# Second mixer: k and b by token in diagonal blocks, and the convolution norm's sums at a later place

## The chip, the cores and the metric

The kernel runs on one core of a Trainium2 chip. The time is the device time of one execution in microseconds (us); the median of several runs is given. A profile of one execution shows what each engine did: TensorE (PE, its weight loads PEld), VectorE (DVE), ScalarE (ACT), GpSimd (POOL) and SyncE (SP), which issues most transfers.

## What is computed

Two transformer blocks over 512 tokens of 1024 channels, and then a third block whose mixer has two branches. The change lies in that mixer. Its branches, cut to what matters:

```python
# branch 1, by head of 64 channels, 16 heads; state S is 64 x 64
S_t = S_{t-1} diag(w_t) + (S_{t-1} (-kk_t)) (kk_t * a_t)^T + v_t k_t^T ;  o_t = S_t r_t
# branch 2: depthwise convolution over 31 tokens, layer norm over the channels, silu
u = glu[..., :1024] * sigmoid(glu[..., 1024:])
u = conv(u, conv_w) + conv_b                      # (512, 1024)
mu = mean(u, -1); var = mean(square(u - mu), -1)
c_out = silu((u - mu) * rsqrt(var + 1e-5) * g + b)
merged = gate0 * (a_out @ w_rwkv_proj) + gate1 * (c_out @ w_conv_proj)
```

## The kernel before

Everything is kept by channel: a tile is 128 channels by 512 tokens, and the mixer goes over 8 such blocks of channels, fc = 0 to 7, two heads in each. `second_mixer` is a software pipeline of nine stages: in stage i, `wkv_proj` of block i (products with `w_in`), `wkv_inputs` of i-1 (decays, k, b), `wkv_inverse` of i-2 and `wkv_chunks` of i-3 are cut into pieces by `yield`, and `interleave` takes the next piece of whichever part is furthest behind its rate. Beside them stand in `branches` the convolutions (`conv_chunk`, eight in stages 0 to 6), the gates (`branch_gate`) and, in stage 8, the convolution's norm and the first of its output products (`conv_out`). A scheduler behind this moves instructions within each engine's queue; so the order on an engine isn't quite that of the code, and every engine and every queue takes its instructions in that order.

`wkv_chunks` solves the recurrence by chunks of 64 tokens, eight steps for a block. A step makes s0 = KA v + AR S (`pair`, two half-array products of 64 x 64, one for each head), sa = `MD` s0 (L1661, a full product: MD holds both heads' inverse in diagonal blocks, zeros beside them), and the next state from k v + b sa (L1667, L1668, two pairs on `ktk` and `btk`, which lie head by head, 64 wide). The outputs gather in `po`: KA v, AR S and, at the step's end, UA sa (L1677). VectorE takes s0, sa and the state out of PSUM between these products.

`wkv_inverse` makes MD: four half-array products per chunk around an inverse of 16 x 16 blocks on VectorE (L1563 to L1568), whose operand goes out to memory (`ud`) and comes back (`ub`), as its result does (`md`, `mn`). Behind it k, b and v are transposed to lie by token (L1586 to L1598).

The convolution's norm: `ConvNorm.add` sums the blocks on GpSimd into `cnsum` and writes them to memory (`cod`). In stage 7 the generator `sums` takes the mean by a product with ones (L1350), then for each of 8 blocks `center`: load into a tile `cacc` of two buffers, subtract on GpSimd (L1357), store (L1358), square on ScalarE (L1359), add into `cnsq` on GpSimd (L1363). `var` is a product with ones again (L1368), a square root and a reciprocal. Both products use the PSUM bank `psd`, which the gates use too. In stage 8 `norm` loads each block again, scales it and writes it over H, the mixer's input, as soon as the gates have read that.

Of the kernel before, what the change touches and what calls it, by code (L numbers as in the profile page):

```python
# [11 lines left out]
F32 = mybir.dt.float32  # L12
# [1112 lines left out]
def second_mixer(g, outer):  # L1125
    nc, tc, d = g.nc, g.tc, g.d
    H = g.X
    with ExitStack() as st:
# [25 lines left out]
        with ExitStack() as s2, ExitStack() as s3, ExitStack() as s4:  # L1154
# [14 lines left out]

            MD = [k1.tile([128, 8, 128], F32, name=f"md{i}") for i in range(2)]  # L1170
            for t in MD:
                nc.gpsimd.memset(t, 0.0)
            parts = [{"MD": MD[i % 2]} for i in range(8)]

# [4 lines left out]
            def sums():  # L1179
                yield 0.0  # L1180
                cn.mean()
                yield 4.0
                for j in range(8):
                    cn.center(j, ka)
                    yield 1.0
                cn.var()

# [15 lines left out]
            def lora():  # L1203

                new = lambda tag, n, bufs: k1.tile([128, n], F32, name=tag, tag=tag, bufs=bufs)
                for blk in range(2):
                    raw = new("ua", 1024, 2).rearrange("p (k n) -> p k n", k=8)
                    nc.sync.dma_start(raw, d["lora1"][:, blk * 128:blk * 128 + 128].rearrange("(k p) n -> p k n", p=128))
                    pss = []
                    for sc in (omm[:, 24:48], vv("mu_lora")):  # L1210
                        w = new("ka", 1024, 2)
                        ws = w.rearrange("p (k n) -> p k n", k=8)
                        for i, (c0, c1) in ((0, (0, 64)), (1, (64, 128))) if blk == 0 else ((2, (0, 128)),):
                            s8 = sc[:, i * 8:i * 8 + 8].unsqueeze(2).to_broadcast([128, 8, c1 - c0])
                            nc.vector.tensor_tensor(ws[:, :, c0:c1], raw[:, :, c0:c1], s8, op=ALU.mult)
                        hi = g.whi.tile([128, 1024], F32R, name="whi", tag="whi")
                        lo = g.wlo.tile([128, 1024], F32R, name="wlo", tag="wlo")
                        split_sb(g, w, hi, lo)
                        ps = g.ps("pst")
                        for kc in range(8):  # L1220
                            o = slice(kc * 128, kc * 128 + 128)
                            mm3(nc, ps, (hi[:, o], lo[:, o]), (H[0][:, kc, :], H[1][:, kc, :]), kc == 0, kc == 7)
                            yield 0.65
                        pss.append(ps)
                    pre, sb = new("oo", 512, 1), new("gate", 512, 1)
                    nc.scalar.copy(sb, pss[1])
                    nc.vector.tensor_copy(pre[:, 0:1], pss[0][:, 0:1])
                    nc.vector.tensor_tensor(pre[:, 1:512], pss[0][:, 1:512], sb[:, 0:511], op=ALU.add)
                    if blk == 0:
                        nc.scalar.activation(pre[0:64], pre[0:64], AF.Tanh)  # L1230
                        for T, o in ((TW, 0), (TA, 64)):
                            own, oth = slice(o, o + 64), slice(64 - o, 128 - o)
                            nc.scalar.activation(T[own], pre[own], AF.Copy)
                            nc.vector.tensor_tensor(T[oth], pre[own], T[own].bitcast(F32), op=ALU.subtract)
                    else:
                        nc.scalar.activation(pre, pre, AF.Tanh, scale=0.5)
                        nc.vector.tensor_scalar(pre, pre, 0.5, 0.5, op0=ALU.mult, op1=ALU.add)
                        split_sb(g, pre, TG[0], TG[1])

            interleave((30.2, wkv_proj(g, 0, parts[0], env)), (16.0, branches(0)), (11.7, lora()))  # L1240
            for i in range(1, 9):
# [5 lines left out]
                if i == SUMS:  # L1247
                    work += [(12.7, sums())]
                interleave(*late, *work[::-1], (n, branches(i)))
# [72 lines left out]
class ConvNorm:  # L1322


    def __init__(self, g, k1, hv, ka):
        self.g, self.hv, self.pool = g, hv, None
        self.early = itertools.cycle([(ka, "cacc", 2), (ka, "cacc", 2), (ka, "glt", 1), (ka, "glu", 1), (ka, "r", 2), (ka, "k", 2)])
        self.sum = k1.tile([128, 512], F32, name="cnsum")
# [24 lines left out]
    def center(self, j, ka):  # L1353
        nc = self.g.nc
        t = ka.tile([128, 512], F32, name="cn", tag="cacc", bufs=2)
        nc.sync.dma_start(t, self.row(j))
# [35 lines left out]
def conv_chunk(g, fc, ka, vv, cw, H, cn):  # L1392
# [11 lines left out]
                         bias=vv("conv_b")[:, fc:fc + 1])  # L1404
    acc = ka.tile([128, 512], F32, name="cacc", tag="cacc", bufs=2)
    for j in range(1, 31):
# [29 lines left out]
def wkv_inputs(g, fc, st, env):  # L1436
# [43 lines left out]
    nc.scalar.activation(kk, k, AF.Copy, scale=col(vv("k_k"), fc))  # L1480
    sq = tmp("tmpa")
    nc.gpsimd.tensor_tensor(sq, kk, kk, op=ALU.mult)
# [8 lines left out]
    nc.vector.reciprocal(rs, rs)  # L1491
    BK = two("bk", (128, 2, 512), 2)
    b = BK[:, 0, :]
# [20 lines left out]
def wkv_inverse(g, fc, st, env):  # L1514
# [72 lines left out]
    for src, nm in ((st["v"], "vtk"), (BK[:, 0, :], "btk"), (BK[:, 1, :], "ktk")):  # L1587
        ps = g.ps("pst")
        for i in range(4):
            nc.tensor.transpose(ps[:, i * 128:i * 128 + 128], src[:, i * 128:i * 128 + 128], g.ident)  # L1590
        t = new(nm, (128, 8, 64), 2)
        p4 = ps.rearrange("p (i h f) -> p i h f", i=4, h=2)
        tv = t.rearrange("p (i e) f -> p i e f", e=2)
        for cp in range(2):
            for hp in range(2):
                nc.scalar.copy(tv[64 * hp:64 * hp + 64, :, cp, :], p4[64 * cp:64 * cp + 64, :, hp, :])
        tok.append(t)
        yield 0.5  # L1598
    bc = lambda m: m.unsqueeze(1).to_broadcast([128, 8, 64])
    for j in (4, 5):  # L1600
# [10 lines left out]
        if j == 5:  # L1611
            for hp in range(2):
                o = slice(64 * hp, 64 * hp + 64)
                nc.vector.tensor_tensor(st["MD"][o, :, o], c3(ps)[o], M[o], op=ALU.add)
        else:
# [12 lines left out]
def wkv_chunks(g, fc, st, env, A=None):  # L1628
# [6 lines left out]
    two = lambda tag, shape=(128, 512), bufs=1: kb.tile(list(shape), F32, name=tag, tag=tag, bufs=bufs)  # L1635
    AR, UA, KA, MD, F, bon = (st[k] for k in ("AR", "UA", "KA", "MD", "F", "bon"))
    gate = new("gate")
# [7 lines left out]
    St = None  # L1645
    sm = lambda tag: k1.tile([128, 64], F32, name=tag, tag=tag, bufs=3)
    pq = lambda: g.ps("psq")[:, 0:64]
    for cc in range(8):
        oc = po[:, cc * 64:cc * 64 + 64]
        ps = pq()  # L1650
        pair(nc, ps, KA[:, cc, 0, :], vt[:, cc, :], True, St is None)
        if St is not None:
            pair(nc, ps, AR[:, cc, 0, :], St, False, True)
        s0 = sm("s0")
        nc.vector.tensor_copy(s0, ps)
        pair(nc, oc, KA[:, cc, 1, :], vt[:, cc, :], True, False)
        if St is not None:
            pair(nc, oc, AR[:, cc, 1, :], St, False, False)
        yield 0.5
        ps = pq()  # L1660
        nc.tensor.matmul(ps, MD[:, cc, :], s0, start=True, stop=True)  # L1661
        sa = sm("sa")
        nc.vector.tensor_scalar_mul(sa, ps, col(st["rs"], cc))
        yield 0.4
        if cc < 7:
            ps = pq()
            pair(nc, ps, kt[:, cc, :], vt[:, cc, :], True, False)  # L1667
            pair(nc, ps, bt[:, cc, :], sa, False, True)  # L1668
            S2 = sm("st")
# [6 lines left out]
            St = S2  # L1676
        pair(nc, oc, UA[:, cc, 1, :], sa, False, True)  # L1677
        yield 0.5


# [18 lines left out]
    for k in range(4):  # L1699
        nc.tensor.transpose(ps[:, k * 128:k * 128 + 128], t[:, k * 128:k * 128 + 128], g.ident)  # L1700
    o = new("oo")
    p4 = ps.rearrange("p (i h f) -> p i h f", i=4, h=2)
# [55 lines left out]
```

## Time and profile before

| what | value |
|---|---|
| median of 3 runs | 2481.47 us (2478.55 to 2486.14) |
| the profiled execution | 2481.95 us |
| its span | 2479.8 us |
| mean granted TensorE clock | 0.984 |
| TensorE, VectorE, ScalarE, GpSimd busy | 95%, 60%, 52%, 42% |

The span reaches from the first to the last instruction of the profile. Of an instruction on the timeline the trace gives its start, its duration, and in brackets how long its engine stood idle ahead of it and what ended that. Matmuls are pipelined: what one costs is read from the distance between two starts, not from its duration. An fp32 product is shown as two passes, so a `pair` has "x4".

### The profile page before, as it was taken

To read this page: it belongs to the slowest core of one execution; us is meant where nothing else is said; L and a number is where in the kernel's file an instruction comes from. 1 tells how busy PE (TensorE), PEld (TensorE's weight loads), DVE (VectorE), ACT (ScalarE), POOL (GpSimd) and SP (SyncE) were. 2 spreads that over 40 slices of the span, in tenths; PEclk is the share of its full clock that TensorE was granted. 3 is DMA by queue.
4 is the path that set the end of the run, shared out by engine and by line. 5 is a ranking of instruction groups with operands and counts; after the bars stand their busy time and mean duration, and the time that the engine had idled before them with its cause. 6 is when DMAs were issued, how large, how long until landed. Compare 5 with 4: busy or idle time off the path is not lost.

```text
span 2479.8 us, 36415 instructions
## 1 busy us (share of the span) xinstructions
PE 2364.9 (95%) x14140; PEld 1898.6 (77%) x14140; DVE 1481.9 (60%) x2782; ACT 1283.0 (52%) x2005; POOL 1030.6 (42%) x571
## 2 busy tenths in 40 slices
PE   8999999999999999999999999999988999899998
PEld 6779778787777787877777877777766679787786
DVE  3776565666443655564685587877756542645556
ACT  5774454445465645444455454666655533544443
POOL 1114677662111025767632232323253114476772
PEclk9999999999999999999999999999998999999999
DMA  7445232347565244232372576666664468232322
GB/s 209 94 141 166 85 116 71 115 121 172 140 136 117 62 124 121 71 119 86 103 202 85 118 167 146 147 144 150 134 173 119 124 172 248 77 102 85 119 81 73
DMA packets 302349, 312.19 MB, mean 126 GB/s; under 512 B 61280, under 2 KB 234976, under 8 KB 302048
## 3 DMA queue, kind: packets, MB, share of 16 engines
q1 hardware_dynamic: 280432, 239.60, 31.9%
q0 software_dynamic: 21168, 68.17, 15.2%
q8 instruction: 111, 1.82, 0.3%
q10 hardware_dynamic: 576, 2.10, 0.2%
q14 instruction: 62, 0.51, 0.1%
HBM read 221.47 MB, written 20.19 MB: 97 GB/s over the span
## 4 chain that ended last, share of the span: by engine, by line
PE 55%; POOL 13%; issue 11%; DVE 9%; DMA 6%; ACT 6%; SPq 0%; POOLq 0%; DVEq 0%; ACTq 0%
PE psm L290 7%; PE psm L291 7%; PE psm L292 7%; POOL wlo L389 4%; PE psa L290 4%; PE psa L291 4%; PE psa L292 4%; POOL wlo L273 3%; DMA wlo<-wraw 2%; PE pst L1416 2%; PE psd L290 2%; PE pss L292 2%; PE pss L291 2%; PE pss L290 2%; PE psd L292 2%
## 5 line engine op out<-in xcount | busy, mean ns | idle before, releaser
L290 PE MATMUL psm<-xT,whi 128*128 128x512 f32 (+1 forms) x1192 | 476.2, 400 | 23.3 <-ACT hf L440 12.3
L292 PE MATMUL psm<-xT,wlo 128*128 128x512 f32 (+1 forms) x1192 | 469.7, 394 | 5.4 <-DMA wlo<-wraw 5.4
L291 PE MATMUL psm<-xT,whi 128*128 128x512 f32 (+1 forms) x1192 | 471.0, 395 | 0.5 <-DVE xT L352 0.5
L267 ACT ACTIVATE whi<-wraw 128x1024 fp32r<-128x1024 f32 (+3 forms) x287 | 285.7, 1005 | 290.8 <-PE psa L292 101.5
L271 POOL DMA_DIRECT2D wlo<-wraw x147 | 127.3, 872 | 729.0 <-ACT wlo L270 497.4
L273 POOL TENSOR_TENSOR wlo<-wraw,whi 128x1024 fp32r<-128x1024 f32 x122 | 315.5, 2620 | 102.0 <-ACT whi L267 73.4
L389 POOL TENSOR_TENSOR wlo<-wraw,whi 128x1024 fp32r<-128x1024 f32 x84 | 212.9, 2534 | 241.9 <-ACT whi L388 241.9
L290 PEld LDWEIGHTS psm<-xT,whi 128*128 128x128 f32 x1192 | 226.7, 190 | 74.7 <-ACT hf L440 13.6
L292 PEld LDWEIGHTS psm<-xT,wlo 128*128 128x128 f32 x1192 | 226.6, 190 | 53.1 <-DMA wlo<-wraw 6.5
L291 PEld LDWEIGHTS psm<-xT,whi 128*128 128x128 f32 x1192 | 227.4, 191 | 44.6 <-DVE xT L352 0.9
L290 PE MATMUL psa<-whi,hh 128*128 128x512 f32 x600 | 239.0, 398 | 15.6 <-DVE x L460 15.5
L291 PE MATMUL psa<-wlo,hh 128*128 128x512 f32 x600 | 236.6, 395 | 0.0
L292 PE MATMUL psa<-whi,hl 128*128 128x512 f32 x600 | 236.4, 395 | 0.0
L388 ACT ACTIVATE whi<-wraw 128x1024 fp32r<-128x1024 f32 x147 | 151.7, 1053 | 123.9 <-PE psa L292 61.8
L1407 DVE SCALAR_TENSOR_TENSOR psc<-glu,cw,psc 128x512 f32<-128x512 f32 x232 | 173.8, 749 | 5.9 <-ACT psc L1403 2.2
L388 ACT ACTIVATE hh<-hf 128x768 fp32r<-128x768 f32 (+1 forms) x96 | 87.8, 914 | 145.2 <-DVE hf L451 143.4
L389 DVE TENSOR_TENSOR hl<-hf,hh 128x768 fp32r<-128x768 f32 (+1 forms) x96 | 124.3, 1295 | 60.2 <-ACT hh L388 60.2
L290 PEld LDWEIGHTS psa<-whi,hh 128*128 128x128 f32 x600 | 112.8, 188 | 49.7 <-DVE x L460 23.1
L389 DVE TENSOR_TENSOR wlo<-wraw,whi 128x1024 fp32r<-128x1024 f32 x63 | 86.4, 1396 | 92.5 <-ACT whi L388 87.8
L270 ACT ACTIVATE wlo<-whi 128x1024 fp32r<-128x1024 f32 (+3 forms) x147 | 140.1, 956 | 2.3 <-PE psm L292 0.7
L292 PEld LDWEIGHTS psa<-whi,hl 128*128 128x128 f32 x600 | 112.8, 188 | 27.2 <-DVE hl L389 0.7
L291 PEld LDWEIGHTS psa<-wlo,hh 128*128 128x128 f32 x600 | 112.8, 188 | 25.8
(464 smaller groups left out, 5208.6 us busy)
## 6 DMA issues: line engine op xcount, KB each, us to landing
wlo<-wraw POOLq DMA_DIRECT2D x123, 512.0 KB, 5.3
wraw<-in_w_up SPq DMA_DIRECT2D x64, 512.0 KB, 4.5
wraw<-in_w_down SPq DMA_DIRECT2D x64, 512.0 KB, 3.6
wraw<-in_w_ff SPq DMA_DIRECT2D x64, 512.0 KB, 3.8
wraw<-in_w_in SPq DMA_DIRECT2D x56, 512.0 KB, 4.9
wraw<-in_od_w_in SPq DMA_DIRECT2D x24, 512.0 KB, 4.3
wraw<-in_ple_w_gate SPq DMA_DIRECT2D x16, 512.0 KB, 4.6
brow<-in_rows SPq DMA_DIRECT2D x13, 512.0 KB, 6.7
```

The lines of the kernel that those rows point to most:

```text
L267: nc.scalar.activation(hi[:, :m], raw[:, :m], AF.Copy)
L270: nc.scalar.activation(lo[:, :m], hi[:, :m].bitcast(F32), AF.Copy, scale=-1.0)
L271: nc.gpsimd.dma_start(lo[:, :m].bitcast(F32), raw[:, :m], accum_op=ALU.add)
L273: eng.tensor_tensor(lo[:, :m], raw[:, :m], hi[:, :m].bitcast(F32), op=ALU.subtract)
L290: nc.tensor.matmul(ps, w[0], x[0], start=first, stop=False)
L291: nc.tensor.matmul(ps, w[0], x[1], start=False, stop=False)
L292: nc.tensor.matmul(ps, w[1], x[0], start=False, stop=last)
L388: g.nc.scalar.activation(hi, src, AF.Copy)
L389: (eng or g.nc.gpsimd).tensor_tensor(lo, src, hi.bitcast(F32), op=ALU.subtract)
L1407: nc.vector.scalar_tensor_tensor(acc if j == 30 else part, u[:, j:j + 512], cw[:, fc * 31 + j:fc * 31 + j + 1], part, op0=ALU.mult, op1=AL ...
L1416: nc.tensor.matmul(ps[o], lhs[o], rhs[o], start=start, stop=stop)
```

## The change

The k and b tiles by token become 128 x 128 diagonal blocks with zeros beside them, kept in two sets as MD is; the products k v and b sa become one full product each. UA sa moves from the end of a step into the next step, behind its AR S products. The pieces of a step are yielded at 0.7, 0.3 and 0.4 instead of 0.5, 0.4 and 0.5. `sums` begins later (a first yield of 2.0), its rate becomes 17.5 and `var` stands 3.0 behind the last block. For space, `cacc` gets one buffer, the small tiles two, `oo` becomes `ot`, and the square of kk lies in `bk`. Line numbers behind L1170 grow by one, and those behind L1592 by two to four.

```diff
-            MD = [k1.tile([128, 8, 128], F32, name=f"md{i}") for i in range(2)]
-            for t in MD:
+            diag = {k: [k1.tile([128, 8, 128], F32, name=f"{k}{i}") for i in range(2)] for k in ("md", "btk", "ktk")}
+            for t in itertools.chain(*diag.values()):
                 nc.gpsimd.memset(t, 0.0)
-            parts = [{"MD": MD[i % 2]} for i in range(8)]
+            parts = [{k: t[i % 2] for k, t in diag.items()} for i in range(8)]
...
             def sums():
-                yield 0.0
+                yield 2.0
                 cn.mean()
                 yield 4.0
                 for j in range(8):
                     cn.center(j, ka)
                     yield 1.0
+                yield 3.0
                 cn.var()
...
-                    work += [(12.7, sums())]
+                    work += [(17.5, sums())]
...
-        self.early = itertools.cycle([(ka, "cacc", 2), (ka, "cacc", 2), (ka, "glt", 1), (ka, "glu", 1), (ka, "r", 2), (ka, "k", 2)])
+        self.early = itertools.cycle([(ka, "cacc", 1), (ka, "glt", 1), (ka, "glu", 1), (ka, "r", 2), (ka, "k", 2)])
...
-        t = ka.tile([128, 512], F32, name="cn", tag="cacc", bufs=2)
+        t = ka.tile([128, 512], F32, name="cn", tag="cacc")
...
-    sq = tmp("tmpa")
+    BK = two("bk", (128, 2, 512), 2)
+    sq = BK[:, 1, :]
...
-        t = new(nm, (128, 8, 64), 2)
+        t = st.get(nm) or new(nm, (128, 8, 64), 2)
...
-                nc.scalar.copy(tv[64 * hp:64 * hp + 64, :, cp, :], p4[64 * cp:64 * cp + 64, :, hp, :])
+                o = slice(64 * hp, 64 * hp + 64)
+                nc.scalar.copy(tv[o, :, cp, o if nm in st else slice(0, 64)], p4[64 * cp:64 * cp + 64, :, hp, :])
...
-    sm = lambda tag: k1.tile([128, 64], F32, name=tag, tag=tag, bufs=3)
+    sm = lambda tag: k1.tile([128, 64], F32, name=tag, tag=tag, bufs=2)
...
         if St is not None:
             pair(nc, ps, AR[:, cc, 0, :], St, False, True)
+            pair(nc, oc(cc - 1), UA[:, cc - 1, 1, :], sa, False, True)
...
-        yield 0.5
+        yield 0.7
...
-        yield 0.4
+        yield 0.3
         if cc < 7:
             ps = pq()
-            pair(nc, ps, kt[:, cc, :], vt[:, cc, :], True, False)
-            pair(nc, ps, bt[:, cc, :], sa, False, True)
+            nc.tensor.matmul(ps, kt[:, cc, :], vt[:, cc, :], start=True, stop=False)
+            nc.tensor.matmul(ps, bt[:, cc, :], sa, start=False, stop=True)
...
             St = S2
-        pair(nc, oc, UA[:, cc, 1, :], sa, False, True)
-        yield 0.5
+            yield 0.4
+    pair(nc, oc(7), UA[:, 7, 1, :], sa, False, True)
...
-    o = new("oo")
+    o = t
```

How this moves instructions, at three places. First TensorE around the mean product, which stood behind the second step's b product of the fifth chunk loop:

```order
L1416 MATMUL psq<-vtk,ktk 64x64 x2
L1416 MATMUL psq<-sa,btk 64x64 x2
L1350 MATMUL psd<-cnsum,ca 128x512
L1416 MATMUL pso<-sa,ua 64x64 x2
L1416 MATMUL pso<-vtk,ka 64x64 x2
```

and now stands behind the last step's AR S product (L1671 and L1672 are the full products on k and b):

```order
L1671 MATMUL psq<-vtk,ktk_11250 128x64
L1672 MATMUL psq<-sa,btk_11248 128x64
L291 MATMUL psd<-xT_62,whi 128x512
L292 MATMUL psd<-xT_61,wlo 128x512
L290 MATMUL psm<-xT_61,whi 128x512
L291 MATMUL psm<-xT_62,whi 128x512
L292 MATMUL psm<-xT_61,wlo 128x512
L1417 MATMUL psq<-vtk,ka 64x64 x2
L1417 MATMUL psq<-st,ar 64x64 x2
L1351 MATMUL psd<-cnsum,ca 128x512
L1417 MATMUL pso<-sa,ua 64x64 x2
L1417 MATMUL pso<-vtk,ka 64x64 x2
```

Six steps of the loop have moved ahead of the mean. Second TensorE around the variance product, before, with the sixth chunk loop (its first step's L1661) behind it:

```order
L1416 MATMUL pst<-mm,yy 64x64 x16
L1416 MATMUL pst<-ar,bk 64x128 x8
L1368 MATMUL psd<-cnsq,ca 128x512
L1661 MATMUL psq<-s_16718,md_11247 128x64
L1474 MATMUL psm<-ta,whi 128x512
```

and now, with that loop's last step (L1665 on `md`), the products of the seventh inverse and then the gates (`psd`, L290 to L292):

```order
L1665 MATMUL psq<-s_17069,md_11247 128x64
L1417 MATMUL pso<-sa,ua 64x64 x2
L1417 MATMUL psq<-vtk,ka 64x64 x2
L1417 MATMUL pso<-vtk,ka 64x64 x2
L1417 MATMUL pst<-mn,ua 64x64 x16
L1703 MATMUL pst<-ca,ot 128x128 x4
L1417 MATMUL pst<-mn,yy 64x64 x16
L1417 MATMUL pst<-yy,mn 64x64 x16
L1417 MATMUL pst<-nn,ua 64x64 x16
L1369 MATMUL psd<-cnsq,ca 128x512
L1417 MATMUL pst<-mm,yy 64x64 x12
L290 MATMUL psd<-xT_61,whi 128x512
```

The whole sixth loop now stands ahead of the variance, with no 512-column product in it. Third SyncE's queue, where the centred blocks were loaded (L1356) and stored (L1358) in twos:

```order
L1356 DMA cn<-cod 128x512 x2
L265 DMA wraw<-in_w_in 128x8x128
L1557 DMA ub<-ud 64x16x16
L1358 DMA cod<-cn 128x512 x2
L1375 DMA cn<-cod 128x512
L1356 DMA cn<-cod 128x512 x2
L1358 DMA cod<-cn 128x512 x2
```

and are now (L1357, L1359) one by one, the last four of them among the transfers of the seventh inverse (`md`, `mn`):

```order
L1357 DMA cn<-cod 128x512
L1359 DMA cod<-cn 128x512
L1357 DMA cn<-cod 128x512
L1573 DMA md<-mb 64x16x16
L1573 DMA md<-nb 64x16x16
L1359 DMA cod<-cn 128x512
L1576 DMA mn<-md 64x8x64 x2
L1357 DMA cn<-cod 128x512
L1576 DMA mn<-md 64x8x64 x2
L1359 DMA cod<-cn 128x512
L1357 DMA cn<-cod 128x512
L1359 DMA cod<-cn 128x512
```

Each load waits there for GpSimd's add of the block before it.

## Rows read from the trace of the kernel before

**Rows 1.** The page, busy time and share of the span by engine.
```profile
PE 2364.9 (95%) x14140; PEld 1898.6 (77%) x14140; DVE 1481.9 (60%) x2782; ACT 1283.0 (52%) x2005; POOL 1030.6 (42%) x571
```

**Rows 2.** Stretches: length, busy us of PE, PEld, DVE, ACT, POOL, then granted clock, DMA.
```profile
1712.00:1790.00 78.00, 77.78 (x732) 58.43 (x732) 58.02 (x151) 47.06 (x80) 21.98 (x21) 1.00 0.66 149
1790.00:1865.00 75.00, 64.00 (x615) 47.50 (x615) 41.57 (x121) 43.51 (x80) 37.27 (x32) 0.92 0.67 171
1865.00:1940.00 75.00, 66.23 (x611) 49.15 (x612) 44.64 (x120) 42.42 (x79) 22.50 (x19) 0.83 0.46 115
...
1861.00:1870.00 9.00, 9.00 (x59) 7.05 (x60) 5.16 (x16) 7.76 (x12) 1.18 (x1) 0.50 0.12 36
```

**Rows 3.** TensorE's timeline: start, us, line, out<-in, idle before and its releaser.
```profile
1803.69 1.12 PE L1350 MATMUL psd<-cnsum,ca 128*128 128x512 f32 x2 [1.81 <-POOL cnsum L1345]
...
1824.25 0.33 PE L1416 MATMUL psq<-vtk,ka 64*64 64x64 f32 x4 [1.85 <-DVE st L1675]
...
1828.05 0.69 PE L1661 MATMUL psq<-s,md 128*128 128x64 f32 x2 [2.69 <-DVE s L1655]
...
1833.83 0.28 PE L1416 MATMUL pso<-vtk,ka 64*64 64x64 f32 x4
...
1860.96 2.07 PE L1368 MATMUL psd<-cnsq,ca 128*128 128x512 f32 x2 [4.10 <-POOL cnsq L1363]
```

**Rows 4.** TensorE's timeline, two chunk steps between 1805 and 1809 us.
```profile
1805.14 0.28 PE L1416 MATMUL psq<-st,ar 64*64 64x64 f32 x4
1805.26 0.28 PE L1416 MATMUL pso<-st,ar 64*64 64x64 f32 x4
1805.50 0.50 PE L290 MATMUL psd<-xT,whi 128*128 128x512 f32 x1
...
1807.69 0.33 PE L1661 MATMUL psq<-s,md 128*128 128x64 f32 x2
1807.83 0.48 PE L290 MATMUL psd<-xT,whi 128*128 128x512 f32 x1
1808.15 0.39 PE L291 MATMUL psd<-xT,whi 128*128 128x512 f32 x1
1808.38 0.40 PE L292 MATMUL psd<-xT,wlo 128*128 128x512 f32 x1
1808.70 0.33 PE L1416 MATMUL psq<-vtk,ktk 64*64 64x64 f32 x4
```

**Rows 5.** GpSimd's timeline.
```profile
1351.21 0.96 POOL L1172 MEMSET md<- 128x1024 f32 x1 [27.36 <-PE psm L347]
...
1819.94 1.27 POOL L1363 TENSOR_TENSOR cnsq<-cnsq,cn 128x512 f32<-128x512 f32 x1 [2.33 <-ACT cn L1359]
...
1855.23 1.26 POOL L1709 TENSOR_TENSOR oo<-oo,bon 128x512 f32<-128x512 f32 x1
```

**Rows 6.** VectorE's timeline.
```profile
1820.11 1.17 DVE L1568 TENSOR_TENSOR mb<-mb,mbt 64x48 f32<-64x48 f32 x1
...
1830.85 0.19 DVE L1568 TENSOR_TENSOR mb<-mb,mbt 64x48 f32<-64x48 f32 x1
...
1958.48 0.69 DVE L1388 SCALAR_TENSOR_TENSOR cn<-cn,psm 128x512 f32<-128x512 f32 x1
```

**Rows 7.** Landing of the centred blocks' loads (L1356), then of their stores (L1358).
```profile
DMA to landing us min/median/max: 2.6/3.5/5.0
...
DMA to landing us min/median/max: 2.0/2.6/5.7
```

**Rows 8.** ScalarE's timeline, the first block's square.
```profile
1811.09 0.63 ACT L1359 ACTIVATE cn<-cn 128x512 f32<-128x512 f32 x1 [5.40 <-DMA cod<-cn]
```

**Rows 9.** SyncE's queue: the seventh inverse's round trip, and the norm's last load.
```profile
1875.40 1.28 SPq L1555 DMA_DIRECT2D ud<-ua  x2
...
1905.48 0.59 SPq L1572 DMA_DIRECT2D md<-mb  x1
...
1947.78 0.33 SPq L1375 DMA_DIRECT2D cn<-cod  x1
```

More of the change, by code (lines that the diff above doesn't have):

```diff
@@ L1224, in lora @@
                         pss.append(ps)
-                    pre, sb = new("oo", 512, 1), new("gate", 512, 1)
+                    pre, sb = new("ot", 512, 1), new("gate", 512, 1)
                     nc.scalar.copy(sb, pss[1])
@@ L1404, in conv_chunk @@
                          bias=vv("conv_b")[:, fc:fc + 1])
-    acc = ka.tile([128, 512], F32, name="cacc", tag="cacc", bufs=2)
+    acc = ka.tile([128, 512], F32, name="cacc", tag="cacc")
     for j in range(1, 31):
@@ L1491, in wkv_inputs @@
     nc.vector.reciprocal(rs, rs)
-    BK = two("bk", (128, 2, 512), 2)
     b = BK[:, 0, :]
@@ L1613, in wkv_inverse @@
                 o = slice(64 * hp, 64 * hp + 64)
-                nc.vector.tensor_tensor(st["MD"][o, :, o], c3(ps)[o], M[o], op=ALU.add)
+                nc.vector.tensor_tensor(st["md"][o, :, o], c3(ps)[o], M[o], op=ALU.add)
         else:
@@ L1635, in wkv_chunks @@
     two = lambda tag, shape=(128, 512), bufs=1: kb.tile(list(shape), F32, name=tag, tag=tag, bufs=bufs)
-    AR, UA, KA, MD, F, bon = (st[k] for k in ("AR", "UA", "KA", "MD", "F", "bon"))
+    AR, UA, KA, MD, F, bon = (st[k] for k in ("AR", "UA", "KA", "md", "F", "bon"))
     gate = new("gate")
@@ L1645, in wkv_chunks @@
     St = None
-    sm = lambda tag: k1.tile([128, 64], F32, name=tag, tag=tag, bufs=3)
+    sm = lambda tag: k1.tile([128, 64], F32, name=tag, tag=tag, bufs=2)
     pq = lambda: g.ps("psq")[:, 0:64]
+    oc = lambda cc: po[:, cc * 64:cc * 64 + 64]
+    sa = None
     for cc in range(8):
-        oc = po[:, cc * 64:cc * 64 + 64]
         ps = pq()
@@ L1653, in wkv_chunks @@
             pair(nc, ps, AR[:, cc, 0, :], St, False, True)
+            pair(nc, oc(cc - 1), UA[:, cc - 1, 1, :], sa, False, True)
         s0 = sm("s0")
         nc.vector.tensor_copy(s0, ps)
-        pair(nc, oc, KA[:, cc, 1, :], vt[:, cc, :], True, False)
+        pair(nc, oc(cc), KA[:, cc, 1, :], vt[:, cc, :], True, False)
         if St is not None:
-            pair(nc, oc, AR[:, cc, 1, :], St, False, False)
-        yield 0.5
+            pair(nc, oc(cc), AR[:, cc, 1, :], St, False, False)
+        yield 0.7
         ps = pq()
```

## Prediction

> **What bounds the kernel now.** I read the engine shares first: TensorE is busy 95% of the span [rows 1], so time can be won only where it waits or runs at its lower clock, or by giving it less work. The table of stretches comes second: up to 1790 us the second mixer keeps TensorE full, and then two stretches of 75 us hold 64.0 and 66.2 us of work, at a mean granted clock of 0.92 and 0.83 [rows 2]. These are the last stages with chunk loops, in which the convolution norm is summed; what the change moves lies there. Third, TensorE's timeline names the waits: for the last add to `cnsum` ahead of the mean product (1.81 us), for an `st` and an `s` of the chunk loop (1.85 and 2.69 us), and for the last add to `cnsq` ahead of the variance product (4.10 us) [rows 3]. After the last one the clock stands at 0.50 for 9 us [rows 2].
>
> The profiled execution took 2481.95 us, 2.15 more than its span and 0.5 above the median of the three runs; the sum is made against 2481.95.
>
> **Full-array products.** Each of 56 chunk steps gives up two pairs of half-array products, for k and for b, and gets two full products. A pair takes 0.12 us of TensorE's time (1805.14 to 1805.26), a full product of the same width 0.14 (the `md` product, 1807.69 to 1807.83) [rows 4]: 112 times 0.02 is 2 us more. What could pay is the change of array shape. A 512-column product is followed after 0.23 us by its like, but after 0.32 by a half-array pair; and behind a pair the next full product starts after 0.24 instead of 0.12 [rows 4]. So a burst of half-array products costs about 0.2 us beside its products. If every step lost one burst, that would be 56 times 0.2 = 11 us. But in the order the `ua` products still stand right behind the b product in most steps, and of 195 bursts 178 are left: 17 times 0.2 = 3.4 us. Together -1 us.
>
> The Trainium skill, TensorEngine Tiling (Array Packing), "Theoretical Speedup", speaks against these products: where contraction and output are at most 64, tiles run side by side, up to 2x for each small dimension. By the row, 112 full products cost 2 us more than the pairs; by that section's 2x they would cost 13 us more. The row decides for the sum, and the rest is a rival below.
>
> **Copies, tiles, memsets.** The copies into the diagonal blocks keep their number and size, 0. `oo` becomes `ot` and `tmpa` a half of `bk`: their former readers are a stage back, 0. Two buffers do for the small tiles, since a step's are last read in the next, 0; the new yields shift a step's pieces by one or two 512-column products, which hide its waits as they did, 0. Four more memsets of 0.96 us follow two on GpSimd, the second of which came after 27.4 us of idle time [rows 5]: the engine has slack there, 0; without that cover at most 4 us.
>
> **The mean, later.** In the order it now stands behind the seventh `st` product of the fifth chunk loop, which ran at 1833.83 before [rows 3]. Its wait goes (1.81), and its own 1.1 us move behind that point. So do the squares: before, GpSimd's adds ran while VectorE made the inverse. There the same instruction took 1.17 us beside such an add (1820.11, the add from 1819.94) and 0.19 without [rows 5, 6], and both chunk waits, 4.5 us, stand in that piece [rows 3]. I take them as mostly gone, and with them 2 us of low clock, an estimate: a mean of 0.92 over 75 us is 6 us lost, of which the 4 us at 0.50 behind the variance make 2 [rows 2], and I give half of the other 4 to these waits. 1833.83 less 1.8, 1.1, 4.5 and 2 is 1824.4; I put the mean at M = 1825. The bounds are 1824 and, with everything still there, 1834.
>
> **One buffer instead of two for the eight centred blocks.** Now a block must be loaded, centred, stored, squared and added before the next load starts: 3.5 + 1.27 + 2.6 + 0.63 + 1.27 = 9.3 us [rows 5, 7, 8]. The bounds by the shortest landings, 2.6 and 2.0, are 7.8, and by landings one third longer about 11. The first two blocks are held up by other work: in GpSimd's order the second add stands behind the two `ot` operations, the `oo` ones of before. These ended 24 us behind the point that is now M (1855.23 + 2 x 1.26 less 1833.83) [rows 3, 5]. Six blocks follow: 24 + 6 x 9.3 = 80 us. On SyncE's queue the sixth block's store stands behind `md` of the next inverse. That inverse's `ud` stands behind the fourth block's load, at M + 33; 30 us from `ud` to `md` (1875.40 to 1905.48) [rows 9] give M + 63, against M + 57 for a store without that: 7 us. So the variance product can run at M + 87 = 1912. It ran at 1860.96 [rows 3].
>
> **What TensorE does meanwhile.** The gate products share the variance's PSUM bank `psd`, so they stand behind it in the order, and the sixth chunk loop, which they filled before, runs bare ahead of it. The filler up to there took 23 us (1833.83 to 1856.9), and eight bare steps take at most 4 us each (1824.25 to 1828.05 is the worst piece [rows 3]): by M + 55 TensorE has little left but four inverse products, and waits some 25 us. But that loop, which took the stretch to 1940 before, is then done.
>
> **After the variance.** Its passes at the low clock and the square root take 4 us; the four gates are 96 products at 0.23 us = 22 us; 9 us of low clock [rows 2] add 4.5; pieces of the next loop between them add 8: the gates end 38 us behind it. Then the norm may overwrite their operand. Its last load stands on SyncE behind `md` of the last inverse, whose `ud` follows the first gate, at about +18: +18 + 30 [rows 9] = +48 or +49. From that load to the first product with the convolution's output 10.7 us passed (1947.78 [rows 9] to 1958.48 [rows 6]): +60. If the queue does not hold it, +49. So that product comes at 1912 + 60 = 1972 instead of 1958.48, 13.5 us later. By then the seventh chunk loop is two steps further than before, 2 us of TensorE's work (a step is five pairs and three full products, 1.0 us). What follows has the same work in the same order.
>
> **Sum:** +13.5 - 2 - 1 = +10.5, so 2492 us. A measurement of this kernel can tell about 0.3%, 7.4 us, from no change.
>
> **Rivals.**
> - *The sums become cover, and the kernel is faster.* The blocks cycle in 7.8 us (-9), `md` isn't late for the sixth store (-7), and the norm isn't held by the last inverse (-11). All three give 2492 - 27 = 2465, two of them 2472 to 2476. For it: the bare loop leaves the DMA queues quieter than the first block's store saw them. Against it: in the order one queue holds all these transfers. It decides once the variance comes before about 1895. Chance 0.22.
> - *Given and taken are equal.* Only one of the three holds: 2481 to 2485. 0.26.
> - *The mean isn't earlier.* M stays at 1834 and the blocks take 11 us: +9 +10, about 2510. For it: a half of the chunk waits may come from the loop itself. 0.14.
> - *Full products at twice a pair.* At 2 x 0.12 = 0.24 instead of 0.14 us, 112 of them add 11 us to the forecast: 2503. Against it: the `md` row, one product of that kind [rows 4]. 0.03. It is the time that the section named above would give.
>
> **How the numbers follow.** The forecast, slower by 8 to 20 us because the one-buffer chain moves the variance by 50 us, has 0.35. Slower in all 0.35 + 0.14 + 0.03 = 0.52, same 0.26, faster 0.22. The forecast's own range is 2490 to 2502. The range to 8 in 10 takes in most of the rivals: 2468 to 2510.
>
> **What would show it.** Right: the variance product at 1905 to 1920, waiting for GpSimd's add for over 10 us; loads of the last blocks 8 to 11 us apart; the low clock there longer than 9 us; the chunk waits near 1825 gone; the `btk` product at about 0.14 us. Wrong: the variance before 1895, or TensorE busy up to it; the first product with the convolution's output before 1958; or a difference that comes from before 1790, where I put less than 1 us.

## The result and the profile after

| kernel | median | against the kernel before |
|---|---|---|
| before | 2482.09 us (2478.55 to 2486.14, 4 runs) | |
| after | 2500.27 us (2498.12 to 2501.89, 4 runs) | 1.0072, 95% interval 1.0055 to 1.0090 |

The change makes the kernel slower by 18 us. The profiled execution took 2501.89 us with a span of 2499.8 us, 20.0 more than before. The page, by engine; compare [rows 1]:

```profile
PE 2374.3 (95%) x13916; PEld 1920.5 (77%) x13916; DVE 1474.8 (59%) x2782; ACT 1283.9 (51%) x2003; POOL 1036.3 (41%) x575
```

TensorE has 224 matmuls fewer, and is yet busy 9.4 us longer, its weight loads 21.9 us. So about half of the 20 us shows as busy time, which includes work at a lower clock (a mean of 0.980 for 0.984), and the rest as waiting. TensorE's timeline has the two products of the sums and the longest wait of the mixer; the rows of before are in [rows 3]:

```profile
1841.42 1.10 PE L1351 MATMUL psd<-cnsum,ca 128*128 128x512 f32 x2 [0.18 <-ACT bgt L1319]
...
1912.82 1.97 PE L1417 MATMUL pst<-mn,ua 64*64 64x64 f32 x32 [14.21 <-DMA mn<-md]
...
1925.12 2.07 PE L1369 MATMUL psd<-cnsq,ca 128*128 128x512 f32 x2 [3.83 <-POOL cnsq L1364]
```

The mean was forecast at 1825 and ran at 1841.4; the variance was forecast at 1912 and ran at 1925.1. Stretches, with the columns of [rows 2]:

```profile
1748.00:1841.00 93.00, 92.05 (x834) 70.26 (x834) 62.63 (x189) 48.76 (x87) 26.92 (x25) 1.00 0.55 125
1841.00:1926.00 85.00, 57.55 (x681) 44.81 (x678) 37.56 (x140) 48.38 (x96) 39.48 (x33) 0.80 0.57 144
1926.00:1985.00 59.00, 56.41 (x410) 43.26 (x410) 33.41 (x82) 30.42 (x52) 15.56 (x12) 0.94 0.40 106
1985.00:2100.00 115.00, 112.64 (x809) 90.33 (x808) 49.47 (x112) 50.16 (x82) 22.96 (x19) 1.00 0.68 200
...
1900.00:1910.00 10.00, 0.00 (x0) 0.00 (x0) 2.59 (x25) 5.48 (x12) 2.52 (x2) 0.50 0.42 95
```

Up to the mean TensorE is full at its full clock: the chunk waits of before are gone from there, as forecast. Behind it stand 85 us with 57.6 us of work, 10 us of them empty at half the clock. SyncE's queue in that stretch:

```profile
1875.60 1.30 SPq L1556 DMA_DIRECT2D ud<-ua  x2
...
1899.97 0.32 SPq L1357 DMA_DIRECT2D cn<-cod  x1
1901.63 0.58 SPq L1573 DMA_DIRECT2D md<-mb  x1
1902.31 0.62 SPq L1573 DMA_DIRECT2D md<-nb  x1
1903.89 0.33 SPq L1359 DMA_DIRECT2D cod<-cn  x1
...
1908.71 0.33 SPq L1357 DMA_DIRECT2D cn<-cod  x1
...
1912.79 0.33 SPq L1359 DMA_DIRECT2D cod<-cn  x1
...
1916.90 0.33 SPq L1357 DMA_DIRECT2D cn<-cod  x1
...
1969.02 0.58 SPq L1573 DMA_DIRECT2D md<-mb  x1
...
1974.39 0.33 SPq L1376 DMA_DIRECT2D cn<-cod  x1
...
1985.29 0.33 SPq L1390 DMA_DIRECT2D cod<-cn  x1
```

`cn<-cod` is a load of a centred block, `cod<-cn` a store. They go load, store, load: one block at a time, 8.2 us from load to load at the end, with the inverse's transfers between them. The norm's last load stands behind `md` of the last inverse, and the first store of the convolution's output (L1390) comes 10.9 us after that load.

To compare kernels, the span is cut in four: from the store of the third convolution block (1492.07 before, 1493.23 after) to the mean product, to the variance product, to the first store of the convolution's output, and to the end. The third block's store itself lies between 1487.9 and 1496.7 in the fourteen profiles, which is left out so. All in us; the ratio is that of the timed runs.

| kernel | to mean | to variance | to output | to end | sum | ratio to before, interval |
|---|---|---|---|---|---|---|
| before | 311.6 | 57.3 | 98.2 | 520.6 | 987.7 | |
| after | 348.2 | 83.7 | 60.2 | 514.5 | 1006.6 | 1.0072 (1.0055 to 1.0090) |
| e1 pairs | 344.4 | 82.3 | 59.6 | 514.4 | 1000.6 | 1.0057 (1.0040 to 1.0073) |
| e2 sums back | 323.2 | 99.9 | 62.1 | 526.6 | 1011.7 | 1.0062 (1.0045 to 1.0080) |
| e3 both | 323.7 | 95.1 | 59.4 | 523.4 | 1001.6 | 1.0060 (1.0041 to 1.0078) |
| e4 one buffer | 311.6 | 94.3 | 58.1 | 525.5 | 989.6 | 1.0013 (1.0000 to 1.0026) |
| e5 order | 323.8 | 58.8 | 85.3 | 519.5 | 987.3 | 1.0004 (0.9992 to 1.0015) |
| e6 old order | 342.2 | 80.9 | 61.9 | 512.7 | 997.8 | 1.0052 (1.0031 to 1.0072) |
| e7 sums late | 332.9 | 49.1 | 73.7 | 521.4 | 977.1 | 0.9966 (0.9953 to 0.9979) |
| e8 variance next | 312.0 | 70.1 | 77.2 | 520.8 | 980.1 | 0.9970 (0.9957 to 0.9983) |
| e9 late, one buffer | 332.9 | 81.7 | 58.8 | 515.7 | 989.2 | 1.0005 (0.9995 to 1.0015) |
| e10 late, order, tail | 337.2 | 51.4 | 76.6 | 522.8 | 988.0 | 0.9997 (0.9983 to 1.0010) |
| e11 late, rings | 334.8 | 48.9 | 73.8 | 522.6 | 980.1 | 0.9966 (0.9954 to 0.9978) |
| e12 b full | 348.9 | 56.7 | 78.8 | 523.3 | 1007.7 | 1.0054 (1.0040 to 1.0068) |

In before, e2 to e5 and e8 the mean stands at its old place in the program, six chunk steps earlier. What the expectations call the third block is the fifth, and e12's fourth and seventh are the third and the eighth.

### The profile page after: what moved, and what is told of

The parts are those of the page before. It is cut to its first block, busy times and chain, and to the rows that moved or that the text cites. A ratio compares the mean times of both kernels' runs of the same rounds, so it can differ in the third digit from the quotient of the medians.

```text
span 2499.8 us, 35994 instructions
## 1 busy us (share of the span) xinstructions
PE 2374.3 (95%) x13916; PEld 1920.5 (77%) x13916; DVE 1474.8 (59%) x2782; ACT 1283.9 (51%) x2003; POOL 1036.3 (41%) x575
## 5 line engine op out<-in xcount | busy, mean ns | idle before, releaser
L290 PE MATMUL psm<-xT,whi 128*128 128x512 f32 (+1 forms) x1192 | 476.8, 401 | 21.5 <-ACT hf L440 11.9
L292 PE MATMUL psm<-xT,wlo 128*128 128x512 f32 (+1 forms) x1192 | 471.5, 396 | 7.1 <-DMA wlo<-wraw 7.1
L290 PEld LDWEIGHTS psm<-xT,whi 128*128 128x128 f32 x1192 | 227.7, 191 | 72.8 <-ACT hf L440 13.2
L292 PEld LDWEIGHTS psm<-xT,wlo 128*128 128x128 f32 x1192 | 227.6, 191 | 55.2 <-DMA wlo<-wraw 8.8
L290 PE MATMUL psa<-whi,hh 128*128 128x512 f32 x600 | 239.0, 399 | 13.8 <-DVE x L460 13.8
L292 PE MATMUL psa<-whi,hl 128*128 128x512 f32 x600 | 236.5, 396 | 0.0
L290 PEld LDWEIGHTS psa<-whi,hh 128*128 128x128 f32 x600 | 112.9, 188 | 47.6 <-DVE x L460 21.1
L292 PEld LDWEIGHTS psa<-whi,hl 128*128 128x128 f32 x600 | 112.8, 188 | 27.3 <-DVE hl L389 0.7
```

Source lines behind the costliest of these rows:

```text
L290: nc.tensor.matmul(ps, w[0], x[0], start=first, stop=False)
L292: nc.tensor.matmul(ps, w[1], x[0], start=False, stop=last)
```

## Experiments

**Parts of the change undone.** e1 puts pairs back, on the diagonal blocks:

```diff
-            nc.tensor.matmul(ps, kt[:, cc, :], vt[:, cc, :], start=True, stop=False)
-            nc.tensor.matmul(ps, bt[:, cc, :], sa, start=False, stop=True)
+            for w, x, first in ((kt, vt[:, cc, :], True), (bt, sa, False)):
+                for hp in (1, 0):
+                    o = slice(64 * hp, 64 * hp + 64)
+                    nc.tensor.matmul(ps[o], w[o, cc, o], x[o], start=first, stop=not first)
```

> The changed kernel with the k and b products as half-array pairs again, on the diagonal blocks of the same tiles; order, yields, sums and the one buffer stay. Theory A (the products are the mis-sized term): in the chunk loops from 1480 to 1845 us TensorE spent 26.2 us on 70 full products by token where the kernel before spent 21.5 on the pairs, 0.067 us more for each, so 112 of them give back 7.5 us: about 2492, and the mean product comes some 5 us sooner than 1841. Theory B (the order and the yields cost what was lost ahead of the mean): 2498 to 2502 and the mean stays at 1841.

The median is 2497.76 us, just below theory B's range and well above theory A's 2492. The mean comes 4.4 us sooner, as theory A has it, and the sum of the stretches is 6 us shorter; of the runs 3.7 us are left, and the two intervals overlap. So in this order full products cost little, if anything, and most of the loss ahead of the mean is not theirs. e2 puts the sums back:

```diff
-                yield 2.0
+                yield 0.0
                 cn.mean()
...
-                yield 3.0
                 cn.var()
...
-                    work += [(17.5, sums())]
+                    work += [(12.7, sums())]
```

> The changed kernel with the sums at their old place (no delay ahead of the mean, none ahead of the variance, 12.7 instead of 17.5); one buffer and full products stay. Theory A (what is lost behind the mean is lost by the later sums): the first product with the convolution's output comes 10 us sooner than 1984, and the time is about 2490. Theory C (the one buffer paces the chain and moving its start wins nothing; the time ahead of the mean is lost anyway): 2497 to 2505.

2499.74 us: theory C. The output does come 7 us sooner behind the third block (485.2 for 492.1), and the end doesn't: behind it 526.6 us follow instead of 514.5. e3 has both edits:

> Both of these undone: half-array pairs and the sums at their old place; what is left of the change is the one buffer, the new order of the ua products with its yields, and the smaller rings. If the two costs add up (7.5 and 10): about 2482, no change from the kernel before. If the one buffer or the order costs by itself: 2490 or more.

2497.96 us. The costs don't add up to the change: without full products and without later sums it is still 15 us slower than before. What is left in e3 is one buffer, the new order, the smaller rings (fewer buffers for the small tiles, and tiles shared) and the diagonal tiles.

**Parts of the change alone, on the kernel before.** e4 has one buffer:

```diff
-        t = ka.tile([128, 512], F32, name="cn", tag="cacc", bufs=2)
+        t = ka.tile([128, 512], F32, name="cn", tag="cacc")
```

and the same for the convolution's own `cacc` and in the list `early`.

> The kernel before with one buffer for the convolution's sums instead of two, nothing else. Theory A (the chain of eight centred blocks needs about 9.3 us a block with one buffer, and the gates stand behind the variance): the variance product comes 30 us or more after 1861, TensorE waits there, 2487 to 2495. Theory D (the gates have slack, only the later start of the sums costs): 2480 to 2484.

2487.08 us, 3 us more, at the low end of theory A; its interval touches 1. The variance came 37 us later, and TensorE waited 10.7 us for it, and yet that costs little: the output product isn't later. e5 has the order:

```diff
             pair(nc, ps, AR[:, cc, 0, :], St, False, True)
+            pair(nc, oc(cc - 1), UA[:, cc - 1, 1, :], sa, False, True)
...
-        yield 0.5
+        yield 0.7
...
-        yield 0.4
+        yield 0.3
...
-        pair(nc, oc, UA[:, cc, 1, :], sa, False, True)
-        yield 0.5
+            yield 0.4
+    pair(nc, oc(7), UA[:, 7, 1, :], sa, False, True)
```

> The kernel before with the chunk loop's order of the change alone: the ua product behind the next step's ar product, yields of 0.7, 0.3 and 0.4 instead of 0.5, 0.4 and 0.5, none behind the last ua product; pairs, tiles, buffers and sums as before. Theory O (the order is the largest term: the loop's last passes come earlier among the other pieces, so ScalarE does them ahead of the weight splits and TensorE waits for wlo near 1570 us): 2489 to 2495, and the store of the third block of the convolution comes some 8 us after 1593. Theory R (the smaller rings, the square in bk and ot in place of oo, cost it): 2481 to 2486.

2481.47 us, no change, and in the trace both theories have a half: the mean comes 12.2 us later, as theory O says, and from the variance to the output 12.9 us are won back. With one buffer nothing is won back there: e3 is e4 with the order, the smaller rings and the diagonal tiles; its mean comes 12.1 us later, and its time is 11.7 us longer by the ratios. The mean is delayed no more than by the order alone, so the rings and the tiles show no cost up to there. Where the loss ahead of the mean arises is shown with e10. e6 is the change with the old order, that is without this edit:

> The changed kernel with the old order and yields of the chunk loop; full products, one buffer, later sums and the smaller rings stay. Theory O: 2488 to 2492, and the mean product comes about 10 us before 1841. Theory R: 2497 to 2502, the mean product within 3 us of 1841.

2493.11 us, 5 us less than the change by the ratios, a little above theory O's range. The mean is 11.3 us before 1841 on the clock of the profile, of which 6.0 lie behind the third block. So the order costs about 5 here, with overlapping intervals, and nothing in e5. e7 has the later sums, with two buffers; the edit is e2's, reversed:

> The kernel before with the sums later alone (2.0 ahead of the mean, 3.0 ahead of the variance, 17.5 instead of 12.7); two buffers, pairs and order as before. Theory A (the variance holds the gates back however many buffers there are): the mean at about 1825, the variance after 1890, 2486 to 2494. Theory D (with two buffers the chain is short enough, and TensorE no longer waits for the sums): the variance before 1890, 2474 to 2482.

2471.16 us: theory D, and somewhat below its range. It is 8 us faster than before and the lowest median here; e8 and e11 below have nearly the same ratio. TensorE's timeline of e7, and of e9 with one buffer:

```profile
1822.50 1.10 PE L1351 MATMUL psd<-cnsum,ca 128*128 128x512 f32 x2 [0.39 <-ACT bgt L1319]
...
1871.60 1.12 PE L1369 MATMUL psd<-cnsq,ca 128*128 128x512 f32 x2
```

```profile
1828.75 1.10 PE L1351 MATMUL psd<-cnsum,ca 128*128 128x512 f32 x2 [0.41 <-ACT bgt L1319]
...
1901.06 1.97 PE L1417 MATMUL pst<-mn,ua 64*64 64x64 f32 x32 [16.77 <-DMA mn<-md]
...
1910.47 1.12 PE L1369 MATMUL psd<-cnsq,ca 128*128 128x512 f32 x2 [1.73 <-POOL cnsq L1364]
```

With two buffers the variance follows the mean by 49 us and TensorE doesn't wait for it. e9 is e7 with e4's edit:

> The later sums of e7 with one buffer instead of two, on the kernel before; pairs, order and rings as before. Theory A (the one buffer makes the chain of centred blocks too long for sums that start late): the mean stays at 1822 as in e7, the variance comes 80 to 88 us behind it, near 1905, instead of 49, TensorE waits 10 us or more, and the time is 2484 to 2492. Theory F (one buffer costs the 3 us that it cost with early sums): 2472 to 2476.

2483.12 us: theory A as to the chain (81.7 us), at the time of before. TensorE waits 16.8 us for the inverse's `mn`, which stands ahead of the variance, and then 1.7 us for the sums themselves. The second buffer alone is worth 0.4%, 10 us, to the later sums; the intervals of e7 and e9 don't overlap. It was given up for the diagonal tiles.

e9 also closes a square. All four kernels in it have later sums and one buffer; e9 has neither the order nor the full products, e1 has the order, e6 the full products, the change both (all but e9 with the rings and the tiles). The mean comes 332.9, 344.4, 342.2 and 348.2 us behind the third block, and the ratios are 1.0005, 1.0057, 1.0052 and 1.0072. So the order alone costs 12.9 us and the full products alone 11.6, both clear of e9's interval, and together they cost 16.6: the two costs overlap, which is why undoing one of them gives back only 4 or 5.

e8 asks whether the variance can simply be later; it is issued behind the first gate of stage 8:

```diff
                     yield 1.0
-                cn.var()
...
                     yield from branch_gate(g, next(gates), ka, "glt", hv, H)
+                    if i == 8 and q == 0:
+                        yield 1.0
+                        cn.var()
```

> The kernel before with the variance product alone moved later: behind the first gate of the last loop instead of ahead of it, so that 24 products of that gate and three chunk steps stand ahead of it. Theory A (the variance has slack up to the first norm, and its wait of 4.1 us and the low clock behind it can be filled): 2473 to 2479. Theory E (the norms then start later and the end moves with them, or the wait is put elsewhere): 2480 to 2488.

2473.78 us, theory A: the wait of 4.10 us [rows 3] is gone, and the kernel is 7 us faster with one line moved.

**The order.** e10 is e7 with e5's edit, and keeps the last yield for all eight steps:

```diff
-            yield 0.4
+        yield 0.4
     pair(nc, oc(7), UA[:, 7, 1, :], sa, False, True)
```

> The later sums of e7 with the new order of the ua products, but with a yield of 0.4 kept behind the eighth step too, so that a loop's last passes stand about where they stood before. Theory G (the new order lost 8 us near 1570 because the shorter loop puts its last passes ahead of the weight splits on ScalarE): the store of the third block comes within 3 us of e7's 1591, and the time is 2467 to 2473. Theory H (the new place of the ua product or the longer first yield does it): the store at 1597 to 1600, as with the order alone.

2482.05 us. Theory G's time is missed. By the clock of the profile the fifth block's store stands at 1598.4, where theory H has it; but in this execution the third block's store already stands 7.1 us later than in e7, and from the third block to the fifth both need the same (101.6 and 101.2 us). So theory G holds for the place. The stretch from the fourth to the fifth block's store, of before, of e5 and of e10, one line each:

```profile
1536.69:1592.95 56.26, 55.21 (x581) 41.94 (x578) 45.49 (x125) 35.01 (x64) 13.29 (x13) 1.00 0.66 148
```

```profile
1534.49:1599.29 64.80, 61.05 (x596) 46.27 (x593) 46.55 (x133) 35.45 (x66) 15.37 (x15) 0.95 0.61 139
```

```profile
1541.84:1598.35 56.51, 55.34 (x587) 42.15 (x582) 45.66 (x127) 34.63 (x65) 13.40 (x13) 1.00 0.66 146
```

With the order alone 8.5 us are lost here: 2.7 more of idle time, 3.2 by the clock (0.05 of 64.8), and the rest is work that moved in. With the tail yield it is back at 56.5. The two products that show why are the decay's, on `whi` and `wlo` of `lora2`; in the kernel before, in e5, and then in e10:

```profile
1567.83 0.47 PE L1450 MATMUL psm<-tw,whi 128*128 128x512 f32 x1 [0.47 <-DVE v L1122]
...
1582.44 0.50 PE L1451 MATMUL psm<-tw,wlo 128*128 128x512 f32 x1
```

```profile
1567.29 0.50 PE L1450 MATMUL psm<-tw,whi 128*128 128x512 f32 x1
1570.05 0.80 PE L1451 MATMUL psm<-tw,wlo 128*128 128x512 f32 x1 [2.26 <-DMA wlo<-wraw]
```

```profile
1573.23 0.47 PE L1451 MATMUL psm<-tw,whi 128*128 128x512 f32 x1 [0.49 <-DVE v L1122]
...
1587.84 0.50 PE L1452 MATMUL psm<-tw,wlo 128*128 128x512 f32 x1
```

Before and in e10 the second product stands 14.6 us behind the first, with filler between, and its weights have landed. In e5, where the loop's pieces are 0.4 shorter in all, it stands right behind the first, and the transfer of its weights is waited for. The change itself has the same pair:

```profile
1572.41 0.49 PE L1451 MATMUL psm<-tw,whi 128*128 128x512 f32 x1 [0.38 <-DVE v L1122]
1575.14 0.80 PE L1452 MATMUL psm<-tw,wlo 128*128 128x512 f32 x1 [2.23 <-DMA wlo<-wraw]
```

e1 and e3 wait there too (2.63 and 0.88 us), and e6 with the old order doesn't. This shows the place and the cause there. That it came from ScalarE's passes ahead of the weight splits, as theory G put it, isn't shown: before and in e10 they stand ahead of them too. The 3 us that e10 still loses on e7 between the fifth and the eighth block, and what it loses behind the mean, stay open.

**Rings and products.** e11 is e7 with the smaller rings:

```diff
-    sq = tmp("tmpa")
+    BK = two("bk", (128, 2, 512), 2)
+    sq = BK[:, 1, :]
...
-    sm = lambda tag: k1.tile([128, 64], F32, name=tag, tag=tag, bufs=3)
+    sm = lambda tag: k1.tile([128, 64], F32, name=tag, tag=tag, bufs=2)
...
-    o = new("oo")
+    o = t
```

> The later sums of e7 with the smaller rings of the change: the square in a half of bk, ot in place of oo, two buffers for the small tiles. Theory O (rings are free, as forecast): 2468 to 2474. Theory R (they hold writers back): 2476 or more, with waits of GpSimd or VectorE for a tile.

2475.43 us, and the ratio of e7: rings are free, theory O. The median lies just above O's range and just below R's; the kernel before, run beside it, stood at 2482.96. e12 adds diagonal `btk` tiles to e11, and leaves k in pairs:

```diff
             pair(nc, ps, kt[:, cc, :], vt[:, cc, :], True, False)
-            pair(nc, ps, bt[:, cc, :], sa, False, True)
+            nc.tensor.matmul(ps, bt[:, cc, :], sa, start=False, stop=True)
```

> The kernel of e11 (later sums, two buffers, smaller rings, old order) with the b products alone full-array on block-diagonal tiles; k stays in pairs, so that the two buffers still fit. Theory P (a full product costs about 0.1 us of TensorE more than a pair, as the changed kernel with the old order stands to the later sums with one buffer, 1.0052 to 1.0005, 11.6 us for 112): 56 of them add 5 to 6 us, 2475 to 2480 or a ratio of 0.998 to 1.000, and the stretch between the fourth and the seventh block's store grows by 3 us over e11's 313. Theory S (a full product is no dearer, as forecast, and what e6 lost came from the lack of the second buffer): a ratio of 0.996 to 0.997.

2497.72 us: neither; 22 us more than e11 (0.0088 of 2482.5), four times theory P. From the third to the eighth block's store e12 needs 11.6 us more than e11, where theory P put 3. The same burst shows it in three kernels, between two products of 512 columns. All three products as pairs (e11):

```profile
1681.44 0.40 PE L292 MATMUL psd<-xT,wlo 128*128 128x512 f32 x1
1681.77 0.33 PE L1417 MATMUL psq<-vtk,ktk 64*64 64x64 f32 x4
1681.93 0.28 PE L1417 MATMUL psq<-sa,btk 64*64 64x64 f32 x4
1682.05 0.28 PE L1417 MATMUL pso<-sa,ua 64*64 64x64 f32 x4
1682.26 0.51 PE L290 MATMUL psm<-xT,whi 128*128 128x512 f32 x1
1682.61 0.40 PE L291 MATMUL psm<-xT,whi 128*128 128x512 f32 x1
```

k and b full (e6):

```profile
1683.97 0.40 PE L292 MATMUL psd<-xT,wlo 128*128 128x512 f32 x1
1684.20 0.33 PE L1669 MATMUL psq<-vtk,ktk 128*128 128x64 f32 x2
1684.37 0.39 PE L1670 MATMUL psq<-sa,btk 128*128 128x64 f32 x2
1684.69 0.33 PE L1417 MATMUL pso<-sa,ua 64*64 64x64 f32 x4
1684.95 0.50 PE L290 MATMUL psm<-xT,whi 128*128 128x512 f32 x1
1685.28 0.40 PE L291 MATMUL psm<-xT,whi 128*128 128x512 f32 x1
```

b alone full, between two pairs (e12):

```profile
1690.89 0.40 PE L292 MATMUL psd<-xT,wlo 128*128 128x512 f32 x1
1691.22 0.33 PE L1417 MATMUL psq<-vtk,ktk 64*64 64x64 f32 x4
1691.48 0.43 PE L1670 MATMUL psq<-sa,btk 128*128 128x64 f32 x2
1691.84 0.33 PE L1417 MATMUL pso<-sa,ua 64*64 64x64 f32 x4
1692.10 0.50 PE L290 MATMUL psm<-xT,whi 128*128 128x512 f32 x1
1692.44 0.40 PE L291 MATMUL psm<-xT,whi 128*128 128x512 f32 x1
```

From the last 512-column product to the second behind the burst: 1.17, 1.31 and 1.55 us. The other bursts of this form show the same where nothing is waited for: 1.15 to 1.16 us in e11 (7 of them), 1.31 to 1.32 in e6 (10 of 11) and 1.54 to 1.55 in e12 (8). Two full products in one piece cost 0.14 a step, 0.07 each; if every one of 56 steps paid that, an estimate, it would be 8 us, beside the 11.6 by which the ratio of e6 exceeds that of e9. A full product between two pairs costs 0.38 a step, and 56 of those would be 21 us, beside the 22 measured.

In the changed kernel some bursts hold the two full products alone, without a pair behind them:

```profile
1611.42 0.39 PE L292 MATMUL psm<-xT,wlo 128*128 128x512 f32 x1
1611.65 0.33 PE L1671 MATMUL psq<-vtk,ktk 128*128 128x64 f32 x2
1611.82 0.39 PE L1672 MATMUL psq<-sa,btk 128*128 128x64 f32 x2
1612.01 0.48 PE L290 MATMUL psd<-xT,whi 128*128 128x512 f32 x1
1612.33 0.39 PE L291 MATMUL psd<-xT,whi 128*128 128x512 f32 x1
```

That is 0.91 us, and the same burst of two pairs in e1 takes 1.04 (1686.53 to 1687.57): here full products are the cheaper ones. With a pair for `ua` and one for KA v behind them they take 1.43 to 1.63, where e1 mostly has 1.27. The two kinds stand about equally often in the change, and this fits how little e1 gave back.

## Why the prediction was right and where it was wrong

The sign and the range were right: 2500.27 for 2492 (2468 to 2510), slower. But the sign is luck. The part that was to cost, later sums with one buffer (+13.5 - 2), is no slower than before as a kernel of its own (e9, 1.0005: its output comes 6.3 us later, and 4.9 are given back), and the part that was put at -1 and 0 cost 16.6 us. The sum of +10.5 has one term that misses by 15 us, and two that miss by 4 us each the other way.

- *The later sums.* The mean at 1825 means 332.9 us behind the third block, and e7 and e9 measured 332.9: the chunk waits near 1825 went, as forecast, and so did what the prediction held to be their cause: in e7 VectorE's `mb` operation of 64x48 takes 0.19 us at 1816.44, with no GpSimd add beside it, for 1.17 before [rows 6]. In the change the mean came at 348.2, which is not theirs.
- *The step that failed: "Together -1 us" for the products, and 0 for the yields.* e9 has the sums and the buffer alone and stands at 1.0005; the change stands at 1.0072. The order and the full products make the difference, 16.6 us. 15.3 us of the stretches are there at the mean, and 11.7 already at the seventh block's store (1747.2 in the change, 254.0 behind the third block's; 242.3 in e9), which lies ahead of 1790, where the prediction had put less than 1.
- *In the products* a row was misread. 0.14 us for the `md` product is the distance to the next start [rows 4], and the 512-column product behind it needs 0.32 instead of 0.23 us to its own next, in the same rows; 0.09 us of its cost stood there. That makes 0.23 for a lone one, and 0.19 in e6's bursts. Nor was the 0.2 us a burst saved in e6: with a pair for `ua` behind two full products, both changes of array shape are still paid. It was saved in the change where k and b stand alone in a burst. The cost measured is 11.6 us by the ratios of e6 and e9, 8 by the burst, and 3.7 in the new order (e1), where the row gave 2. By the Trainium skill, TensorEngine Tiling (Array Packing), "Theoretical Speedup", the estimate was 13 us for 112 full products, as the prediction said. The first of these costs comes near it, the last near the row.
- *In the yields* "which hide its waits as they did" was right for the chunk loop, and wrong for the other parts: each of them moves too when one generator gets shorter, and the decay's second product lost its filler (e5, e10).
- *The one-buffer chain.* M + 87 was forecast, M + 83.7 measured (81.7 in e9). The 7 us for a store held by `md` were not there: the sixth store, behind `nb`'s, followed its load by 3.9 us (1899.97 to 1903.89), the seventh by 4.1 (1908.71 to 1912.79) and the eighth by 4.1. The rest took 4 us more than forecast. TensorE did wait, but 14.2 us of it for the inverse's `mn` in front of the variance, and 3.8 for GpSimd's add, which was to be over 10.
- *After the variance.* +60 was forecast for the first output product; the store behind it came at +60.2. `md` of the last inverse stood ahead of the norm's last load on the queue, as forecast (1969.02, 1974.39).
- *Behind the output product* 2 us were to be given back, and it was 6.1 (520.6 to 514.5), 4.9 in e9. Which work is further on by then, beside the two chunk steps, no run shows.
- In sum: the output came 24.9 us later instead of 13.5 (15.3 by the mean, less 3.9 by the two steps behind it), 6.1 were given back instead of 2, and 1.2 stood ahead of the third block: 20.0, the difference of the spans.
- *The rivals.* "The sums become cover" is what e7 shows, with the second buffer that the change gives up. "Full products at twice a pair" was given 0.03; its cost is, with the order's, what made the kernel slower, but not by a product of twice the time: in one piece a full product costs 0.07 us more than a pair, and the changes of shape do the rest.

## What to carry to other kernels

Price a short product in its whole burst, from the last product at full rate to the second one behind, and count the changes of array shape in it: two full products alone were cheaper than two pairs here, and one between two pairs was the dearest. When a part of an interleaved schedule (a generator) gets shorter, look in the order for what its neighbours lost, above all for a product that now stands right behind the one it was kept apart from. A buffer given up for another part's tiles has its price where the buffer worked: here two buffers and later sums were the gain, and the full products took the buffer away.

## What the runs showed of the hardware

A change of array shape costs TensorE about 0.15 us: e12's burst has two more of them than e11's and one full product instead of a pair, 0.38 - 0.07 = 0.31 us for two. The changed kernel's bursts of k and b alone say the same from the other side: they have no change where e1's have two, and two full products instead of two pairs, 1.04 + 0.14 - 0.91 = 0.27 us for two. The Trainium skill, TensorEngine Tiling (Array Packing), "Key Properties", says that a change of tiling mode drains the engine; it gives no time for it. The bursts agree that each change costs time.

A later variance costs little by itself in this kernel: 37 us later in e4 it moved the time by 3 us, with an interval that touches 1, and 13 us later in e8, with filler ahead of it, the kernel got 7 us faster.
